# First FFN of a decoder layer: the second chunk's norm begun with the first, and weight and operand sums queued on POOL

## The chip, the cores and the metric

The kernel runs on one core of one Trainium2 chip. The metric is the time of one launch in device microseconds. Three runs of the kernel before took 2373.49, 2369.26 and 2369.44 us (median 2369.44). The profiled execution is a run of its own.

## What is computed

One inference step of a decoder layer in float32, for 1024 prompt tokens and 64 sample tokens together (1088 columns, model width 1024):

```python
def swiglu(x, w_gu, w_down):
    gate, up = jnp.split(x @ w_gu, 2, axis=-1)
    return (jax.nn.silu(gate) * up) @ w_down

def macaron_half(x, g_pre, w_gu, w_down, g_post):
    return x + 0.5 * rmsnorm(swiglu(rmsnorm(x, g_pre), w_gu, w_down), g_post)
...
hp = macaron_half(hp, ffn1...)        # first FFN, width 2752
...                                   # projections, two kinds of attention, w_out
hp = macaron_half(hp, ffn2...)        # second FFN
```

The change lies at the start of the first `macaron_half`: its RMS norm over the 1024 rows of a column, and the products with `w_gu` that follow it.

## The kernel before

Activations lie transposed: 8 row blocks of 128 partitions, tokens along the free axis. The 1088 columns are cut in four chunks, `CH` = 256, 256, 256 and 320 columns. The first two are one half (512 columns, tiles `y0` and, normed and split, `ua`), the last two the other (576 columns, `y1` and `ub`). The first FFN runs over the first half (`f1a` in the code) and then over the second (`f1b`).

Each float32 operand of a product is split in two parts, high (`wh`, `uh`, `hh`; a cast on ACT) and low (`wl`, `ul`, `hl`; a subtraction on DVE; in the norm every second row block's on POOL), and a product is three matmuls: high by high, high by low, low by high. The split of weights is `split`, lines 195 and 196. Weights are loaded into two raw buffers (`wr`, line 118) and split into three pairs of buffers, which come free when TensorE has used them. `Feed.pump` loads and splits ahead.

A half begins with `job_first`. For each of its two chunks it makes three products (`gemm`, line 272, 72 matmuls of 256 columns): the tail block of gate and up together, one gate block, one up block. For the first chunk this needs `norm0`, for the second the second chunk's norm. Then come four `down` products (line 530, 40 matmuls of 512 columns in the first half), which need `wt`, a small rearranged piece of the down weights (lines 678 and 679). Their results are copied over `y0` (line 542).

The next blocks are made in `sevens` by a scheme of seven smaller products in place of eight (`seven`, line 591). It needs two kinds of sums. Weight sums are made in `Sums.load` on POOL: three at line 89 and a fourth at line 94 for each block. Operand sums are made in the generator `sevens`, eight for each half at line 666, in place in the normed `y`, each followed by a split into free room: on DVE for the first half, on POOL for the second half (`f.early`), and on DVE for the second FFN's second half (`f3`). They must be through before the `down` results are copied over `y0`.

The norm of a chunk: `rms_quick` squares the eight blocks on ACT and DVE together, adds them to three partial sums, and TensorE adds these over partitions into `ncol` (line 323). The usual way is `square` (lines 282, 286 and 288) and line 301. `rms_col` makes the mean on DVE (line 331) and the power on POOL (line 332); `rms_diag` (343) and `rms_rows` (350) spread the result over partitions; then each block is scaled (412), cast (414) and its low part taken (415). Only the first chunk goes by `rms_quick`; the second is loaded whole in `first1` and its squares are begun after the first chunk's scaling was written.

The order of work on an engine is that in which a scheduler of the compiler issues what is written, moved by its own model of times; each engine then runs its queue strictly in order. `issue_after(x)` holds back instructions behind instruction x if they are on x's engine, and has no effect on other engines. Side work (`beside`) is written between matmuls at set distances.

Of the kernel before, what the change touches and what calls it, by code (L numbers as in the profile page):

```python
# [51 lines left out]
def run(g):  # L52
    for _ in g:
        pass
# [13 lines left out]
class Sums:  # L68
# [8 lines left out]
    def load(self, s):  # L77
        if self.first is self:
# [8 lines left out]
            for out, a, b, op in ((y[:, lo], a21, z[:, hi], ALU.add), (x[:, hi], y[:, lo], x[:, lo], ALU.subtract),  # L87
                                  (y[:, hi], x[:, lo], a21, ALU.subtract)):
                nc.gpsimd.tensor_tensor(out=out, in0=a, in1=b, op=op)  # L89
            self.tiles = [(x, 2 * h), (y, 2 * h), (z, 2 * h), (s4, h)]  # L90
# [7 lines left out]
class Feed:  # L98
# [8 lines left out]
    def _raw(self):  # L107
# [8 lines left out]
        for p in pieces:  # L116
            n = p.shape[-1]
            nc.sync.dma_start(t[:, o:o + n], p)
            o += n
        self.raws.append((t, o))  # L120

    def _split(self):
# [44 lines left out]
class Step:  # L167
# [136 lines left out]
    def rms_quick(self, y, n, pool):  # L304

        nc = self.nc
        wn = windows(n)
        col = self.ptile("col2")[:, :8]
        sq = []
        for k in range(KB):  # L310
# [7 lines left out]
            for a, b in ((0, 2), (1, 3), (4, 5), (6, 7), (6, 4)):  # L318
                if k == max(a, b, 7 * (a == 6)):
                    (nc.vector if a else nc.gpsimd).tensor_tensor(out=sq[a], in0=sq[a], in1=sq[b], op=ALU.add)  # L320
        for i in (0, 1, 6):
            for j, o in enumerate(wn):
                nc.tensor.matmul(col[:, 2 * j:2 * j + 2], sq[i][:, o:o + P], self.ones[:, :2], start=(i == 0 and j == 0), stop=(i == 6 and j == len(wn) - 1))
        return self.rms_col(col, len(wn), pool)

    def rms_col(self, col, m, pool):

        nc = self.nc
        v = pool.tile([P, 4], F32, name=self.uid("nv"), tag="nv", bufs=6)
        vs = v[:, :m]  # L330
        nc.vector.tensor_scalar(vs, col.rearrange("p (j c) -> p j c", c=2)[:, :m, 0], 1.0 / D, EPS, op0=ALU.mult, op1=ALU.add)
        nc.gpsimd.tensor_tensor(out=vs, in0=vs, in1=self.mhalf[:, :m], op=ALU.pow)
        return vs
# [24 lines left out]
    def norm(self, y, y0, c0, n, pool, post=None, pre=None, v=None, key=None):  # L358
# [49 lines left out]
        for k in range(KB):  # L408
# [5 lines left out]
            nc.scalar.copy(uh, yk)  # L414
            (nc.gpsimd if k % 2 else nc.vector).tensor_tensor(out=ul, in0=yk, in1=uh.bitcast(F32), op=ALU.subtract)
        self.ready.add((key, c0))
# [21 lines left out]
    def ffn(self, w_gu, w_dn, f):  # L438
# [216 lines left out]
        def sevens():  # L655
# [7 lines left out]
            for nm, out, p, q in (("t1", b11, b12, b11), ("t3", b12, b22, b12), ("t2", b22, b22, b11), ("t4", b21, b21, b22)):  # L663
                for h in (slice(0, 2), slice(2, 4)):
                    with self.tc.issue_after(self.mark):
                        (nc.gpsimd if f.early else nc.vector).tensor_tensor(out=out[:, h], in0=p[:, h], in1=q[:, h], op=ALU.subtract)
                    yield 1.0
# [519 lines left out]
class StepB(StepA):  # L1187
# [428 lines left out]
    def whole(self):  # L1616
# [21 lines left out]
        for k, m in ((0, 2), (2, 2), (4, 4)):  # L1638
            nc.sync.dma_start(y0[:, k:k + m, :CH[0][1]], A["xT"][:, k:k + m, :CH[0][1]])
        nc.sync.dma_start(self.gain, A["gains"])  # L1640
        for i in (1, 5):
            nc.vector.tensor_scalar(self.gain[:, i, :], self.gain[:, i, :], 0.5, None, op0=ALU.mult)
# [19 lines left out]
        def first1(i):  # L1662
            if i == 0:
                c0, n = CH[1]
                nc.sync.dma_start(y0[:, :, c0:c0 + n], A["xT"][:, :, c0:c0 + n])
                self.load_a()
                run(norm0)
            self.need(("f1", CH[i][0]))
            if i == 0:
                self.beside(self.norm(y0, 0, *CH[1], F, pre=0, key="f1"))  # L1670

# [120 lines left out]
        def after2(c0, n, v):  # L1792
# [14 lines left out]
                  after=lambda c0, n, v: self.norm(p4.y, HALF, c0, n, p4.R, (5, self.h2, O["yT"]), None, v))  # L1807

        sums(f3, flata, lambda: p3.y, lambda: self.need(("o", CH[1][0])))
        f3.first = lambda i: self.need(("f2", CH[2 + i][0]))  # L1810

        def start5():
# [3 lines left out]
            self.px, _ = self.pool("px", keep=True, space=PSUM)  # L1816
        norm0 = self.norm(y0, 0, *CH[0], F, pre=0, key="f1", v=[self.rms_quick(y0, CH[0][1], F)])
        next(norm0)
# [99 lines left out]
```

## Time and profile before

| | before |
|---|---|
| runs, median of 3 (lowest to highest) | 2369.44 us (2369.26 to 2373.49) |
| profiled execution, time | 2357.24 us |
| its span | 2355.5 us |
| TensorE (PE) busy | 2260.2 us, 96% |
| DVE busy | 1558.4 us, 66% |
| ACT busy | 1035.5 us, 44% |
| POOL busy | 710.1 us, 30% |

The profiled execution takes 1.7 us more than its span, and it is 12.2 us shorter than the median of the runs. Busy times of engines overlap. Time without work on TensorE lies mostly at the span's start, at the changes from one part to the next, and at the end.

### The profile page before, as it was taken

How to read it: one execution, taken by the hardware profiler on the slowest of the kernel's cores; microseconds unless marked ns; L12 is line 12 of the kernel's file. 1: busy time of each engine (PE TensorE's matmuls, PEld its weight loads, DVE VectorE, ACT ScalarE, POOL GpSimd, SP SyncE). 2: the span in 40 equal slices, each digit the busy share in tenths (PEclk: the TensorE clock that was granted, in tenths of full speed). 3: DMA queues.
4: the chain of work that ended last, by engine and by line, in shares of the span. 5: the costliest groups of instructions: out<-in, count | busy, mean ns of one | idle time of the engine just before them, and what ended most of it. 6: DMA issues, size and time to landing. Idle time of an engine off the chain costs nothing.

```text
span 2355.5 us, 41285 instructions
## 1 busy us (share of the span) xinstructions
PE 2260.2 (96%) x15512; PEld 2006.8 (85%) x15512; DVE 1558.4 (66%) x2723; ACT 1035.5 (44%) x1786; POOL 710.1 (30%) x658
## 2 busy tenths in 40 slices
PE   6999999999999989999999999999999998999997
PEld 5999988999999869999997666667777988999997
DVE  7888867877777774566465332339675689778765
ACT  5444434533344555755454222226556555334332
POOL 3444415433323221011124444631010135333402
PEclk8999999999999999999999999999999999999998
DMA  4332333322234556664357998865555544433212
GB/s 148 103 97 94 98 122 115 100 89 90 90 105 143 167 191 207 187 199 138 106 184 247 331 316 295 278 190 154 145 156 149 188 157 157 148 95 99 81 59 85
DMA packets 203337, 359.40 MB, mean 153 GB/s; under 512 B 27969, under 2 KB 105858, under 8 KB 202882
## 3 DMA queue, kind: packets, MB, share of 16 engines
q1 hardware_dynamic: 191474, 318.48, 43.4%
q0 software_dynamic: 11664, 38.28, 4.7%
q8 instruction: 123, 2.02, 0.4%
q14 instruction: 76, 0.62, 0.1%
HBM read 311.02 MB, written 45.65 MB: 151 GB/s over the span
## 4 chain that ended last, share of the span: by engine, by line
PE 65%; DVE 16%; issue 6%; ACT 5%; DMA 5%; POOL 3%; SPq 1%; DVEq 0%; POOLq 0%; ACTq 0%
PE mm L272 21%; PE mm L530 17%; PE mm L591 16%; DVE wl L196 6%; ACT wh L195 2%; DMA wr<-in_wout 2%; PE po L1084 2%; PE po L1294 1%; PE sp L1046 1%; PE tp L1278 1%; PE pa L1427 1%; DVE y L606 1%; PE mx L591 1%; DMA y<-in_xT 1%; DMA wr<-in_wgu 1%
## 5 line engine op out<-in xcount | busy, mean ns | idle before, releaser
L272 PE MATMUL mm<-ua,wh 128*128 128x512 f32 (+2 forms) x1712 | 461.1, 358 | 9.0 <-ACT wh L195 6.0
L196 DVE TENSOR_TENSOR wl<-wr,wh 128x1024 fp32r<-128x1024 f32 (+1 forms) x257 | 298.3, 1161 | 169.1 <-ACT wh L195 166.7
L195 ACT CAST wh<-wr 128x1024 fp32r<-128x1024 f32 (+1 forms) x257 | 250.1, 974 | 298.8 <-PE mm L272 101.7
L272 PEld LDWEIGHTS mm<-ua,wh 128*128 128x128 f32 (+1 forms) x1712 | 293.0, 193 | 66.8 <-issue 25.0
L530 PE MATMUL mm<-hh,wh 128*128 128x320 f32 (+2 forms) x974 | 326.9, 339 | 13.7 <-DVE y L544 6.0
L530 PE MATMUL mm<-hl,wh 128*128 128x256 f32 (+2 forms) x1022 | 336.8, 331 | 0.3 <-DVE hl L196 0.2
L272 PE MATMUL mm<-ub,wh 128*128 128x320 f32 (+2 forms) x1600 | 334.9, 304 | 2.0 <-DVE y L544 2.0
L530 PE MATMUL mm<-hh,wl 128*128 128x320 f32 (+2 forms) x974 | 320.4, 330 | 0.9 <-DVE wl L196 0.9
L272 PE MATMUL mm<-ua,wl 128*128 128x512 f32 (+1 forms) x848 | 294.5, 348 | 1.1 <-DVE wl L196 1.1
L591 PE MATMUL mm<-ub,wh 128*128 128x288 f32 (+1 forms) x1392 | 269.9, 290 | 0.9 <-DVE sg L606 0.9
L272 PEld LDWEIGHTS mm<-ub,wh 128*128 128x128 f32 (+1 forms) x1600 | 256.4, 189 | 9.4 <-issue 7.9
L272 PE MATMUL mm<-ub,wl 128*128 128x320 f32 (+1 forms) x784 | 233.0, 297 | 0.7 <-DVE wl L196 0.7
L544 DVE TENSOR_TENSOR y<-y,mm 128x320 f32<-128x320 f32 (+2 forms) x291 | 143.1, 519 | 128.6 <-PE mm L530 128.2
L591 PEld LDWEIGHTS mm<-ub,wh 128*128 128x128 f32 x1392 | 220.8, 189 | 1.1 <-issue 1.1
L530 PEld LDWEIGHTS mm<-hh,wh 128*128 128x128 f32 x974 | 185.1, 191 | 40.0 <-DVE y L544 9.1
L591 PE MATMUL mm<-ua,wh 128*128 128x288 f32 (+1 forms) x1104 | 215.0, 290 | 3.2 <-DVE up L606 2.4
L530 PEld LDWEIGHTS mm<-hl,wh 128*128 128x128 f32 x1022 | 195.5, 191 | 15.0 <-issue 1.3
L591 PE MATMUL mm<-ub,wl 128*128 128x288 f32 (+1 forms) x696 | 201.8, 290 | 0.0
L530 PEld LDWEIGHTS mm<-hh,wl 128*128 128x128 f32 x974 | 185.5, 191 | 16.8 <-DVE wl L196 2.6
L89 POOL TENSOR_TENSOR y<-y,wz 128x512 f32<-128x512 f32 x52 | 68.6, 1319 | 427.9 <-DVE wl L196 422.2
L272 PEld LDWEIGHTS mm<-ua,wl 128*128 128x128 f32 x848 | 163.3, 193 | 22.0 <-DVE wl L196 2.0
L591 PEld LDWEIGHTS mm<-ua,wh 128*128 128x128 f32 x1104 | 175.4, 189 | 4.1 <-DVE up L606 2.6
(299 smaller groups left out, 4331.3 us busy)
## 6 DMA issues: line engine op xcount, KB each, us to landing
wr<-in_wgu SPq DMA_DIRECT2D x68, 512.0 KB
wr<-in_wd SPq DMA_DIRECT2D x64, 512.0 KB
pr<-in_ck SPq DMA_DIRECT2D x112, 256.0 KB
wz<-in_wgu SPq DMA_DIRECT2D x104, 256.0 KB
wr<-in_win SPq DMA_DIRECT2D x50, 512.0 KB
wr<-in_wout SPq DMA_DIRECT2D x32, 512.0 KB
y<-in_wgu SPq DMA_DIRECT2D x52, 256.0 KB
wx<-in_wgu SPq DMA_DIRECT2D x52, 256.0 KB
```

The costliest lines, as they stand in the source:

```text
L89: nc.gpsimd.tensor_tensor(out=out, in0=a, in1=b, op=op)
L195: self.keep(self.nc.scalar.copy(hi, src))
L196: self.keep(self.nc.vector.tensor_tensor(out=lo, in0=src, in1=hi.bitcast(F32), op=ALU.subtract))
L272: nc.tensor.matmul(out, a, x[:, k, o:o + n], start=(k == 0 and j == 0), stop=(k == KB - 1 and j == len(ops) - 1))
L530: nc.tensor.matmul(pds[key], a, x, start=(i == 0 and j == 0), stop=(i == len(g) - 1 and j == len(ops) - 1))
L544: nc.vector.tensor_tensor(out=yk, in0=yk, in1=pds[d2, c0, e], op=ALU.add)
L591: nc.tensor.matmul(ps, a, x, start=(k == 0 and j == 0), stop=(k == KB // 2 - 1 and j == len(ops) - 1))
L606: add = lambda out, x, y: self.keep(nc.vector.tensor_tensor(out=out, in0=x, in1=y, op=ALU.add))
L1046: nc.tensor.matmul(sp[32 * a:32 * a + 32, 256 * hf:256 * hf + 256], qz[p % 2][:, a, s, :], raw[:, :, a * P:(a + 1) * P], start=False, stop ...
L1084: nc.tensor.matmul(po[r], pT[:, t, r], raw[:, :, a * P:(a + 1) * P], start=(t == 0), stop=False)
L1278: nc.tensor.transpose(tp[:, k * P:(k + 1) * P], p[:, (k0 + k) * P:(k0 + k + 1) * P], self.ident)
L1294: nc.tensor.matmul(out, v[:, k, r], pT[:, k, s], start=(k == 0 or (k == 1 and not one)), stop=(k == last or (k == last - 1 and not one)))
```

## The change

The second chunk's columns are loaded right behind the first weight block, in two transfers of four row blocks. `rms_quick` is cut in two: squares and partial sums are written at once, and the rest (matmuls over partitions, mean, power) is a function `finish`, called after the first two blocks of the first chunk are scaled. DVE's part of the second chunk's squares is held behind the first chunk's mean. The weight sums on POOL are held behind `low`, the last low part of the newest norm, which is a POOL instruction. The operand sums of both halves of the first FFN go to POOL behind the same instruction; those of `f3` stay on DVE, where `low` holds nothing.

```diff
 # Sums.load, Feed._raw
+                with s.tc.issue_after(s.low):
+                    nc.gpsimd.tensor_tensor(out=out, in0=a, in1=b, op=op)
...
+        s.behind_raw.pop(len(self.raws), lambda: None)()
...
 # rms_quick
-        for i in (0, 1, 6):
-            for j, o in enumerate(wn):
-                nc.tensor.matmul(col[...], sq[i][:, o:o + P], self.ones[:, :2], ...)
-        return self.rms_col(col, len(wn), pool)
+        def finish():
+            col = self.ptile("col2")[:, :8]
+            ...                                   # the same matmuls
+            return self.rms_col(col, len(wn), pool)
+        return finish
...
 # rms_col, norm
+        self.mean = nc.vector.tensor_scalar(vs, ...).ins
...
+            low = (nc.gpsimd if k % 2 else nc.vector).tensor_tensor(out=ul, ...)
+        self.low = low.ins
...
 # sevens
-                    with self.tc.issue_after(self.mark):
-                        (nc.gpsimd if f.early else nc.vector).tensor_tensor(out=out[:, h], ...)
+                    with self.tc.issue_after(self.mark), self.tc.issue_after(self.low):
+                        (nc.vector if f is self.third else nc.gpsimd).tensor_tensor(out=out[:, h], ...)
...
 # whole
+        def fetch1():
+            c0, n = CH[1]
+            for k in (0, 4):
+                nc.sync.dma_start(y0[:, k:k + 4, c0:c0 + n], A["xT"][:, k:k + 4, c0:c0 + n])
+        self.behind_raw = {1: fetch1}
...
         def first1(i):
             if i == 0:
+                self.load_a()
                 c0, n = CH[1]
-                nc.sync.dma_start(y0[:, :, c0:c0 + n], A["xT"][:, :, c0:c0 + n])
-                self.load_a()
+                with tc.issue_after(self.mean):
+                    finish = self.rms_quick(y0[:, :, c0:c0 + n], n, F)
+                next(norm0)
+                next(norm0)
+                norm1 = self.norm(y0, 0, *CH[1], F, pre=0, key="f1", v=[finish()])
+                next(norm1)
                 run(norm0)
+                self.beside(norm1)
             self.need(("f1", CH[i][0]))
-            if i == 0:
-                self.beside(self.norm(y0, 0, *CH[1], F, pre=0, key="f1"))
```

## Rows read from the trace of the kernel before

**Rows 1.** The page's busy line: busy us, share of the span, instructions.
```profile
PE 2260.2 (96%) x15512; PEld 2006.8 (85%) x15512; DVE 1558.4 (66%) x2723; ACT 1035.5 (44%) x1786; POOL 710.1 (30%) x658
```

**Rows 2.** TensorE by stretch: us, length, busy (matmuls), granted clock, DMA share, GB/s.
```profile
14.50:23.50 9.00, 8.83 (x57) 1.00 0.79 242
...
54.80:61.20 6.40, 6.31 (x21) 0.73 0.07 26
```

**Rows 3.** TensorE's timeline: start, busy us, instruction, count, idle before and releaser.
```profile
22.92 0.40 PE L272 MATMUL mm<-ua,wh 128*128 128x256 f32 x2
23.16 0.28 PE L272 MATMUL mm<-ua,wl 128*128 128x256 f32 x1
26.20 0.58 PE L301 MATMUL ncol<-ones,ss 128*128 128x2 f32 x4 [2.76 <-DVE ss L286]
...
29.79 1.22 PE L350 MATMUL nrows<-dg,ones 128*128 128x128 f32 x4 [1.60 <-DVE dg L343]
...
44.68 0.47 PE L530 MATMUL mm<-hh,wt 128*128 128x512 f32 x1 [2.36 <-DVE wt L679]
...
54.89 0.47 PE L530 MATMUL mm<-hh,wt 128*128 128x512 f32 x1 [3.78 <-DVE wt L679]
...
60.95 0.39 PE L530 MATMUL mm<-hh,wl 128*128 128x512 f32 x1
61.19 0.39 PE L591 MATMUL mm<-ua,wh 128*128 128x256 f32 x2
```

**Rows 4.** POOL's timeline, 22 to 37 us.
```profile
22.91 1.46 POOL L89 TENSOR_TENSOR y<-y,wz 128x512 f32<-128x512 f32 x1
...
28.57 0.71 POOL L332 TENSOR_TENSOR nv<-nv,mhalf 128x2 f32<-128x2 f32 x1
...
35.94 0.74 POOL L415 TENSOR_TENSOR ua<-y,ua 128x256 fp32r<-128x256 f32 x1 [0.31 <-ACT ua L414]
```

**Rows 5.** DVE's timeline, 18 to 65 us.
```profile
18.89 1.83 DVE L415 TENSOR_TENSOR ua<-y,ua 128x256 fp32r<-128x256 f32 x2
...
31.05 1.26 DVE L412 SCALAR_TENSOR_TENSOR y<-y,gain,nrows 128x256 f32<-128x256 f32 x3 [1.32 <-PE nrows L350]
...
54.45 0.49 DVE L679 CAST wt<-wl 64x256 fp32r<-64x256 f32 x2
...
62.28 2.17 DVE L196 TENSOR_TENSOR wl<-wz,wh 128x1024 fp32r<-128x1024 f32 x1 [1.55 <-ACT wh L195]
```

**Rows 6.** Groups by line and shape, DVE's L666 from 20 to 62 us, the others whole.
```profile
L666 DVE TENSOR_TENSOR y<-y 128x512 f32<-128x512 f32 x8 | 5.8, 731 | 0.0
...
L196 DVE TENSOR_TENSOR wl<-wx,wh 128x1024 fp32r<-128x1024 f32 x52 | 63.4, 1218 | 8.6 <-ACT wh L195 8.6
...
L89 POOL TENSOR_TENSOR y<-wx,y 128x512 f32<-128x512 f32 x52 | 102.5, 1971 | 0.6 <-DMA wx<-in_wgu 0.6
L89 POOL TENSOR_TENSOR wx<-y,wx 128x512 f32<-128x512 f32 x52 | 89.1, 1713 | 0.1
L89 POOL TENSOR_TENSOR y<-y,wz 128x512 f32<-128x512 f32 x52 | 68.6, 1319 | 427.9 <-DVE wl L196 422.2 <-issue 4.8 <-DMA y<-in_wgu 0.9
L94 POOL TENSOR_TENSOR y<-wz,wx 128x512 f32<-128x512 f32 x52 | 68.4, 1316 | 74.2 <-issue 40.0 <-POOL wx L89 25.2 <-DMA wz<-in_wgu 4.9
L666 POOL TENSOR_TENSOR y<-y 128x576 f32<-128x576 f32 x8 | 13.2, 1666 | 0.5
```

**Rows 7.** The second half's start, from the timelines of TensorE, POOL and ACT.
```profile
383.21 1.97 PE L530 MATMUL mm<-hh,wh 128*128 128x512 f32 x4 [2.01 <-ACT hh L195]
...
395.83 1.54 POOL L415 TENSOR_TENSOR ub<-y,ub 128x320 fp32r<-128x320 f32 x1 [1.06 <-ACT ub L414]
397.45 3.81 POOL L666 TENSOR_TENSOR y<-y 128x576 f32<-128x576 f32 x2
...
420.74 1.05 ACT L195 CAST wh<-wx 128x1024 fp32r<-128x1024 f32 x1
```

**Rows 8.** A later stretch: us, length, busy of PE, PEld, DVE, ACT, POOL; clock, DMA.
```profile
1300.00:1350.00 50.00, 49.74 (x327) 32.21 (x325) 16.06 (x24) 14.21 (x19) 24.48 (x24) 1.00 0.93 323
```

More of the change, by code (lines that the diff above doesn't have):

```diff
@@ L88, in load @@
                                   (y[:, hi], x[:, lo], a21, ALU.subtract)):
-                nc.gpsimd.tensor_tensor(out=out, in0=a, in1=b, op=op)
+                with s.tc.issue_after(s.low):
+                    nc.gpsimd.tensor_tensor(out=out, in0=a, in1=b, op=op)
             self.tiles = [(x, 2 * h), (y, 2 * h), (z, 2 * h), (s4, h)]
@@ L307, in rms_quick @@
         wn = windows(n)
-        col = self.ptile("col2")[:, :8]
         sq = []
@@ L320, in rms_quick @@
                     (nc.vector if a else nc.gpsimd).tensor_tensor(out=sq[a], in0=sq[a], in1=sq[b], op=ALU.add)
-        for i in (0, 1, 6):
-            for j, o in enumerate(wn):
-                nc.tensor.matmul(col[:, 2 * j:2 * j + 2], sq[i][:, o:o + P], self.ones[:, :2], start=(i == 0 and j == 0), stop=(i == 6 and j == len(wn) - 1))
-        return self.rms_col(col, len(wn), pool)
+        def finish():
+            col = self.ptile("col2")[:, :8]
+            for i in (0, 1, 6):
+                for j, o in enumerate(wn):
+                    nc.tensor.matmul(col[:, 2 * j:2 * j + 2], sq[i][:, o:o + P], self.ones[:, :2], start=(i == 0 and j == 0), stop=(i == 6 and j == len(wn) - 1))
+            return self.rms_col(col, len(wn), pool)
+        return finish
     def rms_col(self, col, m, pool):
@@ L330, in rms_col @@
         vs = v[:, :m]
-        nc.vector.tensor_scalar(vs, col.rearrange("p (j c) -> p j c", c=2)[:, :m, 0], 1.0 / D, EPS, op0=ALU.mult, op1=ALU.add)
+        self.mean = nc.vector.tensor_scalar(vs, col.rearrange("p (j c) -> p j c", c=2)[:, :m, 0], 1.0 / D, EPS, op0=ALU.mult, op1=ALU.add).ins
         nc.gpsimd.tensor_tensor(out=vs, in0=vs, in1=self.mhalf[:, :m], op=ALU.pow)
@@ L414, in norm @@
             nc.scalar.copy(uh, yk)
-            (nc.gpsimd if k % 2 else nc.vector).tensor_tensor(out=ul, in0=yk, in1=uh.bitcast(F32), op=ALU.subtract)
+            low = (nc.gpsimd if k % 2 else nc.vector).tensor_tensor(out=ul, in0=yk, in1=uh.bitcast(F32), op=ALU.subtract)
+        self.low = low.ins
         self.ready.add((key, c0))
@@ L664, in sevens @@
                 for h in (slice(0, 2), slice(2, 4)):
-                    with self.tc.issue_after(self.mark):
-                        (nc.gpsimd if f.early else nc.vector).tensor_tensor(out=out[:, h], in0=p[:, h], in1=q[:, h], op=ALU.subtract)
+                    with self.tc.issue_after(self.mark), self.tc.issue_after(self.low):
+                        (nc.vector if f is self.third else nc.gpsimd).tensor_tensor(out=out[:, h], in0=p[:, h], in1=q[:, h], op=ALU.subtract)
                     yield 1.0
@@ L1807, in whole @@
                   after=lambda c0, n, v: self.norm(p4.y, HALF, c0, n, p4.R, (5, self.h2, O["yT"]), None, v))
+        self.third = f3
         sums(f3, flata, lambda: p3.y, lambda: self.need(("o", CH[1][0])))
@@ L1816, in start5 @@
             self.px, _ = self.pool("px", keep=True, space=PSUM)
-        norm0 = self.norm(y0, 0, *CH[0], F, pre=0, key="f1", v=[self.rms_quick(y0, CH[0][1], F)])
+        norm0 = self.norm(y0, 0, *CH[0], F, pre=0, key="f1", v=[self.rms_quick(y0, CH[0][1], F)()])
         next(norm0)
```

## The prediction

> **What bounds the kernel now.** I read the page first. TensorE is busy for 96% of the span and no other engine for more than 66% [rows 1], so what a change is worth is the time in which TensorE stands still, or runs at its lower clock, and no longer does. I then read TensorE's timeline, wait by wait, at the two places that the diff touches.
>
> At the start of the first half its matmuls begin to flow at about 14.5 us, run without a gap to 23.44 us, and then stop four times [rows 2, 3]: 2.76 us for the second chunk's sums of squares, 1.60 us for the diagonal of its root, and 2.36 and 3.78 us for `wt`, DVE's cast of a piece of the down weights. Each stop also costs clock: in the 6.4 us behind the last one the granted clock is 0.73 [rows 2], a mixture of 1.2 and 2.4 GHz, with TensorE idle before it. The first of the seven products starts at 61.19 us [rows 3]. That start is my yardstick: whatever it moves is the gain of this stage.
>
> POOL's timeline shows why the second chunk is late. Four weight sums are queued from 22.91 us on, and the power of that chunk's mean starts only behind them, at 28.57 us; the last POOL split of the chunk ends at 36.68 us [rows 4]. DVE's timeline has the scaling of that chunk beginning at 31.05 us, though the first chunk's last split on DVE ended at 20.72 us [rows 5]. So some ten microseconds lie between the two chunks.
>
> **The change part by part.** *The second chunk's norm.* Its squares take no new work: five on ACT, three on DVE and four sums, in place of a chain of eight squares and seven sums. What the trace can't show is when they fit. The first chunk's DVE queue has its last split ending at 20.72 us; I add one split of a weight block, 1.22 us [rows 6], because the first weight load to come behind the new transfers lands later and its split then falls among the scaling. Lower bound of this cost nothing, upper bound that split. The second chunk's scaling then starts near 21.9 us. From the start of its scaling to its last POOL split it took 36.68 - 31.05 = 5.63 us [rows 4, 5], so `low` ends at about 27.6 us, 9.1 us sooner than before.
>
> *TensorE's bound.* It had done 57 of the first chunk's matmuls at 23.44 us [rows 2, 3]. With no wait, 15 more and the second chunk's 72 follow at 0.12 us (two in 0.24 us, 22.92 to 23.16) [rows 3]: 10.4 us. The new sum over partitions has 12 matmuls, at 0.58 / 4 us each 1.7 us; spreading the root takes 1.2 us [rows 3]. That puts the end of the six products at 36.8 us. The 40 down matmuls at 0.24 us (60.95 to 61.19) [rows 3] take 9.6 us: 46.4 us.
>
> *Weight and operand sums on POOL.* The eight operand sums were 5.8 us of DVE [rows 6]. POOL takes 1.666 us for 576 columns, so I estimate 1.48 us for 512, 11.9 us for eight. The four weight sums have means of 1.32, 1.71, 1.97 and 1.32 us, together 6.3 us [rows 6]. All twelve stand behind `low`: 27.6 + 18.2 = 45.8 us. If the operand sums go first, the first seven-product still needs the weights cast and split, 1.05 us on ACT [rows 7] and 1.22 us on DVE [rows 6]: 48.1 us. If the weight sums go first, the operands come last; what then waits is the copy of the down products over `y0`, with TensorE's banks behind it, to about the same time. POOL's bound is later than TensorE's by 1.7 us, so I take it: 48.1 us in place of 61.19 us, a gain of 13.1 us. At the uncontended 1.32 us for all twelve POOL would end at 43.4 us, and TensorE's 46.4 us would count: 14.8 us.
>
> *`wt`.* Where two casts stood behind other DVE work until 54.45 us [rows 5], DVE now has 5.8 us less to do. I cost this wait at nothing; the cover is that DVE room, and the price if it is gone is rival A.
>
> *The second half.* Its operand sums were on POOL already, mixed with the chunk's low parts; the last two ended at 401.26 us. Now all eight stand behind the last low part, which ended at 397.37 us [rows 7]: 8 x 1.67 = 13.3 us, to 410.7 us, and the weight sums 6.3 us more, to 417.0 us. The cast of these weights stood at 420.74 us [rows 7], so there are 3.7 us of room. On the other side, TensorE waited 2.01 us at 383.21 us for ACT [rows 7], whose queue had an operand's cast that waited for POOL; that goes, if ACT no longer meets a late sum there. From a gain of 2.0 us to a loss of 9.4 us (410.7 - 401.3), I take nothing, by the room.
>
> *Transfers.* The second chunk's megabyte goes ahead of the second weight block. That block serves the second product, and the squares need the chunk; the 1.22 us above is what I charge. SP's later loads shift with it and are taken up by the wait behind `low`. The holds in the second FFN's second half cost nothing: its operand sums stay on DVE, and its weight sums already follow the norm.
>
> *Does the gain last?* Where DMA is busiest, at 0.93, TensorE still works 49.74 of 50 us [rows 8]: nothing there is tied to a fixed time, so an earlier start moves it all.
>
> **Sum.** 13.1 us from the profiled execution's 2357.24 us gives 2344.1 us. The runs lie 12.2 us above that execution; I subtract the same gain from their median, 2369.44 us: 2356.3 us.
>
> **Rivals.** *A: DVE gets no room, and the `wt` waits stay.* POOL's sums slow DVE's subtractions of two operands beside them: the split of `wz` at 62.28 us took 2.17 us where one beside an idle POOL takes 1.22 us [rows 5, 6]. Eight moved sums that each hold up one such split cost DVE 8 x 0.95 = 7.6 us for the 5.8 us saved. The stage from the last of the six products to the first seven-product then stays 61.19 - 42.32 = 18.9 us (42.32 is 44.68 less its wait) [rows 3], from 36.8 us on: 55.7 us, a gain of 5.5 us, 2363.9 us. Against it speaks the second half, where sums on POOL stand beside `wt` with no such gap. The Trainium skill, "SBUF — State Buffer", section "Who interferes with whom", says that a DVE instruction with two SBUF inputs contends with a GpSimd instruction that reads SBUF, since both need a read interface that is locked for a whole instruction; the 2.17 us row agrees, and by that rule A would be the likeliest case.
>
> *B: the change doesn't bring the second chunk forward.* If its partial sums stand behind the first chunk's scaling on DVE and the root comes as late as now, only the order on POOL changes: 36.68 + 18.2 + 2.3 = 57.2 us, a gain of 4.0 us, 2365.4 us. For it: DVE is full from 14 to 21 us. Against it: only about 3 us of DVE work is asked for, and the first chunk's root leaves a hole before its scaling.
>
> *C: slower. ACT and DVE, in order, stand behind POOL's sums.* In the second half they would meet sums 9.4 us later than now, or 15.7 us if the weight sums go first, with TensorE's results waiting in its banks for the same two engines. In the first half the down products would start only behind the sums, at 45.8 us, and end at 55.4 us, a gain of 5.8 us. The net is 3.6 to 9.9 us slower; at the middle 6.8 us, 2376.2 us. It decides when the second half's stop exceeds 10.5 us (5.8 and the 4.7 us that can be told). Against it: the order is made with the sums' times in view.
>
> **How the numbers follow.** Within 0.2%, 4.7 us, a measurement of this kernel can't tell a change. Forecast 0.58 (its own range 2352 to 2360 us), A 0.16, B 0.14, C 0.12. A lies less than a microsecond inside the bound for faster, so I count 0.10 of it as faster and 0.06 as same. Faster 0.68, same 0.20, slower 0.12. The range goes down to 2350 us (TensorE's bound, the 2.0 us of the second half and some 2 us more, for the rewarmed clock there) and up to 2370 us, no change at all; C lies above it.
>
> **What would show it.** Right: `ncol` of the second chunk by line 323 with a wait under 1 us, its scaling from about 22 us, line 666 on POOL after 27 us, the `wt` waits gone, and line 591 starting at 46 to 50 us. A shows as waits for `wt` with DVE splits near 1 us longer; B as scaling after 28 us; C as ACT or DVE waiting on line 666 with TensorE waiting for them, above all from 397 to 425 us. The prediction is wrong if line 591 starts early but the span does not shrink with it.

## The result, and the profile after

The changed kernel is slower. Its median is 2380.81 us (2372.05 to 2385.72, 20 runs) against 2373.88 us (2367.47 to 2378.19, 20 runs) for the kernel before on the same chip: a ratio of 1.0031 [1.0023, 1.0039], that is 7.4 us more [5.5, 9.3] (the medians stand 6.9 us apart), where 13.1 us less were forecast.

The two profiled executions stand 27.5 us apart (2384.71 and 2357.24 us), and that distance is not the effect. A second profiled execution of the kernel before, below, took 2369.97 us: 12.7 us more than its first, with the same program. From 460 us on, every engine has its instructions in the same order before and after. So I read the two places that the change touches, each by its own length.

The yardstick of the prediction, the first of the seven products (line 591 before, 596 after), starts at 62.64 us in place of 61.19 us [rows 3]. TensorE's timeline of the kernel after, with idle time and releaser in brackets:

```profile
12.80 1.01 PE L326 MATMUL ncol<-ones,sq 128*128 128x2 f32 x4 [2.67 <-POOL sq L321]
15.78 1.02 PE L326 MATMUL ncol<-ones,sq 128*128 128x2 f32 x4 [0.26 <-DVE sq L321]
16.66 2.10 PE L274 MATMUL mm<-ua,wh 128*128 128x256 f32 x4
24.55 0.60 PE L354 MATMUL nrows<-dg,ones 128*128 128x128 f32 x4
43.39 0.76 PE L535 MATMUL mm<-hh,wt 128*128 128x512 f32 x1 [3.76 <-DVE wt L684]
46.35 0.76 PE L535 MATMUL mm<-hh,wt 128*128 128x512 f32 x1 [0.92 <-DVE wt L684]
52.21 1.22 PE L535 MATMUL mm<-hh,wh 128*128 128x512 f32 x2 [4.24 <-ACT hh L197]
62.64 0.40 PE L596 MATMUL mm<-ua,wh 128*128 128x256 f32 x2
...
416.18 0.55 PE L535 MATMUL mm<-hh,wt 128*128 128x256 f32 x1 [3.02 <-DVE wt L684]
...
429.97 0.42 PE L596 MATMUL mm<-ub,wh 128*128 128x288 f32 x2
```

The two stops for the second chunk's norm (2.76 and 1.60 us [rows 3]) are gone, as meant. The six products end at 43.39 - 3.76 = 39.63 us in place of 42.32. All of that, and more, is given back at the down matmuls: three stops of 8.92 us, where two of 6.14 us were, and some 1.4 us more in the matmuls between and behind the stops. The last of the three names a new releaser, ACT's cast `hh`. POOL's timeline shows what moved in beside these matmuls:

```profile
32.59 0.74 POOL L419 TENSOR_TENSOR ua<-y,ua 128x256 fp32r<-128x256 f32 x1 [0.31 <-ACT ua L418]
33.29 4.43 POOL L671 TENSOR_TENSOR y<-y 128x512 f32<-128x512 f32 x3
37.68 1.74 POOL L90 TENSOR_TENSOR y<-y,wz 128x512 f32<-128x512 f32 x1
...
46.02 5.89 POOL L671 TENSOR_TENSOR y<-y 128x512 f32<-128x512 f32 x4
...
392.62 12.92 POOL L671 TENSOR_TENSOR y<-y 128x576 f32<-128x576 f32 x8
```

The twelve sums stand as one block behind `low`, from 33.29 to 51.91 us. ACT's timeline shows who stands behind them: of the eight casts of these operands six wait for their sums, and `hh`, which needs no sum, comes only at 51.75 us, behind four that waited.

```profile
26.13 1.28 ACT L461 ACT_TABLE_LOAD   x1
...
44.42 0.62 ACT L197 CAST ub<-y 128x512 fp32r<-128x512 f32 x1 [3.61 <-POOL y L671]
47.37 0.62 ACT L197 CAST ub<-y 128x512 fp32r<-128x512 f32 x1 [2.03 <-POOL y L671]
...
50.71 0.62 ACT L197 CAST ub<-y 128x512 fp32r<-128x512 f32 x1 [1.05 <-POOL y L671]
51.75 0.40 ACT L197 CAST hh<-sg 128x256 fp32r<-128x256 f32 x1
...
402.78 0.67 ACT L197 CAST ua<-y 128x576 fp32r<-128x576 f32 x1 [0.72 <-POOL y L671]
403.48 0.38 ACT L461 ACTIVATE sg<-mm 64x256 f32<-64x256 f32 x1
```

ACT's list of waits from 30 to 60 us (total, times, longest) sums them up:

```profile
ACT ub L197 <- POOL y L671: 10.0, 6, 3.6
```

DVE's timeline has the third effect. Its subtractions of two operands that both lie in SBUF take about twice their time beside most of POOL's sums: 1.77 us at 36.49 us, where 0.69 us is usual (one, at 41.30 us, took 0.68 us there too). Even the small cast `wt` takes 1.26 us. `sg`, with one operand from TensorE (`mm`), keeps its 0.42 us. The cast in the profile before:

```profile
44.24 0.29 DVE L679 CAST wt<-wl 64x256 fp32r<-64x256 f32 x1
```

DVE in the profile after:

```profile
22.75 0.41 DVE L419 TENSOR_TENSOR ua<-y,ua 128x256 fp32r<-128x256 f32 x1
25.19 1.26 DVE L416 SCALAR_TENSOR_TENSOR y<-y,gain,nrows 128x256 f32<-128x256 f32 x3 [2.03 <-PE nrows L354]
...
36.49 1.77 DVE L198 TENSOR_TENSOR wl<-wr,wh 128x512 fp32r<-128x512 f32 x1
...
41.98 1.26 DVE L684 CAST wt<-wl 64x256 fp32r<-64x256 f32 x1
...
46.24 0.42 DVE L466 TENSOR_TENSOR sg<-mm,sg 128x256 f32<-128x256 f32 x1
...
403.89 0.43 DVE L466 TENSOR_TENSOR sg<-mm,sg 64x256 f32<-64x256 f32 x1 [6.62 <-ACT sg L461]
...
415.75 0.29 DVE L684 CAST wt<-wl 64x256 fp32r<-64x256 f32 x1
```

The same rows show `sg`, the operand of `hh`, done at 46.66 us: ACT's cast of it stood 5.1 us in its queue.

The second half has one block too, eight sums from 392.62 to 405.54 us, with the activation `sg` behind casts that wait for them, DVE idle for 6.62 us until that `sg`, and a new stop of TensorE, 3.02 us, at 416.18 us. The length from the last matmul that spreads the second half's root (line 350 before, 376.71 us; 378.37 us after) to that half's first seven-product was 49.53 us; it is 51.60 us now. The same places in the profile before, of ACT, DVE and TensorE:

```profile
401.99 0.38 ACT L456 ACTIVATE sg<-mm 64x256 f32<-64x256 f32 x1
```
```profile
412.55 0.76 DVE L679 CAST wt<-wl 64x256 fp32r<-64x256 f32 x1
```
```profile
413.77 0.28 PE L530 MATMUL mm<-hh,wt 128*128 128x256 f32 x1
```

Counted from the root, `sg` is not later: 25.3 us before, 25.1 us after. But `wt` ends at 36.6 us before and 37.7 us after, because the same thirteen DVE instructions from `sg` to `wt` take 12.2 us in place of 10.9 us: more of them run beside POOL's sums. TensorE, on its side, reaches these matmuls sooner, at 34.8 us in place of 37.1 us, as the stop of 2.01 us for `hh` [rows 7] is gone. So it stops for `wt`, and from that stop to the seven-product it takes 13.8 us, where it took 12.5 us, at a granted clock of 0.78 in place of 1.00.

So the profile of after shows 1.45 us lost in the first half's opening and 2.07 us in the second's.

### The profile page after: what moved, and what is told of

It reads as the page before. It is cut to its first block, busy times and chain, and to the rows that moved or that the text cites. A ratio compares the mean times of both kernels' runs of the same rounds, so it can differ in the third digit from the quotient of the medians.

```text
span 2382.9 us, 41300 instructions
## 1 busy us (share of the span) xinstructions
PE 2272.4 (95%) x15520; PEld 2011.9 (84%) x15520; DVE 1558.5 (65%) x2717; ACT 1035.0 (43%) x1783; POOL 726.2 (30%) x665
## 3 DMA queue, kind: packets, MB, share of 16 engines
q1 hardware_dynamic: 191490, 318.48, 42.6%
q8 instruction: 123, 2.02, 0.4%
## 4 chain that ended last, share of the span: by engine, by line
PE 63%; DVE 15%; issue 7%; DMA 5%; ACT 5%; POOL 3%; SPq 1%; another core or an unknown queue 1%; DVEq 0%; POOLq 0%; ACTq 0%
PE mm L274 19%; PE mm L535 17%; PE mm L596 15%; DVE wl L198 5%; ACT wh L197 2%; PE po L1089 2%; DMA wr<-in_wout 1%; PE po L1299 1%; PE sp L1051 1%; PE tp L1283 1%; PE pa L1432 1%; DVE y L611 1%; PE mx L596 1%; POOL y L671 1%; DMA y<-in_xT 1%
```

## The experiments

Each kernel ran beside the kernel before on the same chip; the ratios are to that. Times in the table are of each kernel's one profiled execution, in us: *first* is the start of the first seven-product, *second* the length just defined, and *load* the distance from the issue of the second half's columns to the third weight cast on ACT behind it, which enters late in the series.

| kernel | first | second | load | ratio [95%] |
|---|---|---|---|---|
| before | 61.19 | 49.53 | 11.56 | |
| before, again | 61.00 | 49.53 | 10.48 | one run |
| after | 62.64 | 51.60 | 11.71 | 1.0031 [1.0023, 1.0039] |
| after, again | 63.12 | 52.83 | 12.48 | 1.0041 [1.0027, 1.0056] |
| 1 operand sums back | 61.42 | 49.56 | 12.55 | 1.0017 [1.0003, 1.0031] |
| 2 norm alone | 58.02 | 49.59 | 13.1 | 0.9999 [0.9988, 1.0011] |
| 3 sums and hold alone | 62.35 | 51.37 | 10.51 | 1.0020 [1.0008, 1.0033] |
| 4 hold alone | 65.23 | 49.53 | 11.06 | 1.0007 [0.9995, 1.0020] |
| 5 after without the hold | 58.33 | 51.02 | 12.92 | 1.0016 [1.0005, 1.0026] |
| 6 norm, `wt` on POOL | 54.69 | 49.56 | 12.63 | 0.9981 [0.9971, 0.9991] |
| 7 hold, sums as fills | 59.74 | 49.54 | 11.93 | one run |
| 8 second half's sums back | 61.61 | 49.54 | 12.68 | one run |
| 10 as 6, one transfer | 53.24 | 49.54 | 12.53 | 0.9980 [0.9966, 0.9994] |
| 11 as 6, mean late | 56.05 | 49.51 | 12.5 | 0.9986 [0.9976, 0.9995] |
| 12 early transfer alone | 59.87 | 49.53 | 12.01 | 1.0004 [0.9989, 1.0019] |
| 13 norm, old transfer | 56.91 | 49.53 | 10.69 | 0.9985 [0.9971, 0.9999] |
| 14 `wt` on POOL alone | 55.74 | 49.57 | 12.13 | 0.9986 [0.9975, 0.9998] |
| 15 13 and 14 | 54.54 | 49.54 | 10.65 | 0.9977 [0.9962, 0.9993] |

*First* varies by 0.2 to 0.5 us between two executions of one kernel, *second* by nothing before and by 1.2 us after.

**1: the operand sums as before; norm and weight hold stay.**

```diff
-with self.tc.issue_after(self.mark), self.tc.issue_after(self.low):
-    (nc.vector if f is self.third else nc.gpsimd).tensor_tensor(...)
+with self.tc.issue_after(self.mark):
+    (nc.gpsimd if f.early else nc.vector).tensor_tensor(...)
```

> The changed kernel with the operand sums placed as before the change (first half on DVE, second half on POOL, neither held behind the norm); the early norm and the held weight sums stay. Theory T (the loss comes from ACT's and DVE's queues, which run in order and stand behind operand sums that POOL makes late): the 4.2 us stop of TensorE for a cast of the last hidden block goes, the second half is no longer 2.3 us later, the first seven-product starts at 52 to 57 us, and the time falls below before by 4 to 9 us. Rival R (the early norm itself costs: its sums over partitions stand in front of the first products, and its squares push back the first chunk's scaling): the first seven-product starts at 60 us or later and the time is within 2 us of before or above it.

The second half came back whole (49.56 us), so its loss is the operand sums'. The first half did not: 61.42 us, where 52 to 57 had been expected. The operand sums alone were not what kept the early norm from paying.

**2: the norm alone (1, and the weight sums not held).**

```diff
-                with s.tc.issue_after(s.low):
-                    nc.gpsimd.tensor_tensor(out=out, in0=a, in1=b, op=op)
+                nc.gpsimd.tensor_tensor(out=out, in0=a, in1=b, op=op)
```

> Only the early norm and the early load of the second chunk, on the kernel before; no sum on POOL is moved or held. T: the second chunk is scaled earlier, but the weight sums may stand in front of its power on POOL, 5.7 us at most; first seven-product at 52 to 60 us, 2 to 9 us faster than before, and not faster than with the weight sums held. R: no gain, first seven-product at 60 us or later.

58.02 us: 3.2 us sooner than before, and 3.4 us sooner than 1, where no gain over 1 was expected. The hold is what 1 lost: 1 has a stop of 3.36 us for `wt` at 42.27 us, behind four DVE instructions that are each some 1.1 us longer, and 2 has none there. A stop for `wt` of 4.96 us stays in both:

```profile
51.32 0.77 PE L534 MATMUL mm<-hh,wt 128*128 128x512 f32 x1 [4.96 <-DVE wt L683]
58.02 0.39 PE L595 MATMUL mm<-ua,wh 128*128 128x256 f32 x2
```

The runs don't show the 3.2 us: 0.9999.

**3: operand sums and hold, with the norm as before.** On the kernel before:

```diff
 # Sums.load, Feed._raw, norm: as 4, below
 ...
 # sevens
-with self.tc.issue_after(self.mark):
-    (nc.gpsimd if f.early else nc.vector).tensor_tensor(...)
+with self.tc.issue_after(self.mark), self.tc.issue_after(self.low):
+    (nc.vector if f is self.third else nc.gpsimd).tensor_tensor(...)
```

> Only the sums: the operand sums of both halves on POOL behind the last low part, the weight sums held there too, with the norm as before the change. T: slower than before by 3 to 9 us, the second half 2 us later than before by itself, and in the first half ACT waiting for line 666 on POOL with TensorE waiting for ACT. R: no more than 1 us of difference from before in either half, since the cost would lie in the early norm.

Slower without any early norm: 62.35 and 51.37 us, 1.0020. ACT waits 7.7 us for POOL's sums, as expected, but TensorE does not stop for ACT there: it waits 6.10 us for `wt` and 2.65 us for `hl`, both DVE's.

**4: the weight hold alone.** On the kernel before. The order on DVE and ACT stays that of the kernel before, and on TensorE only the matmuls that spread the second chunk's root change their place among the products.

```diff
 # Sums.load, Feed._raw
-                nc.gpsimd.tensor_tensor(out=out, in0=a, in1=b, op=op)
+                with s.tc.issue_after(s.low):
+                    nc.gpsimd.tensor_tensor(out=out, in0=a, in1=b, op=op)
...
 # norm
+            low = (nc.gpsimd if k % 2 else nc.vector).tensor_tensor(out=ul, ...)
+        self.low = low.ins
```

> Only the weight sums held behind the last low part of the norm, nothing else. The power of the second chunk's mean no longer stands behind four weight sums. T: it comes up to 5 us sooner, the 1.6 us stop for the diagonal shrinks, and the first seven-product starts 1 to 5 us sooner. R (POOL's order does not matter there, since the second chunk's sums of squares set the time): less than 1 us.

A gain of 1 to 5 us was expected, and the stage lost 4.0 us: 65.23 us. There was little to gain: in the profile before, DVE's mean of the second chunk (the line below) ended only at 27.66 us, and the power ran at 28.57 us [rows 4], so the weight sums held it up by 0.9 us and no more. It runs at 27.67 us here.

```profile
27.50 0.16 DVE L331 TENSOR_SCALAR nv<-ncol 128x2 f32<-128x2 f32 x1
```

Four sums that moved from 23 to 28.6 us to 36.0 to 42.6 us did that alone. TensorE, POOL and DVE of this kernel:

```profile
47.50 0.76 PE L532 MATMUL mm<-hh,wt 128*128 128x512 f32 x1 [6.45 <-DVE wt L681]
...
65.23 0.39 PE L593 MATMUL mm<-ua,wh 128*128 128x256 f32 x2
```
```profile
36.01 1.74 POOL L90 TENSOR_TENSOR y<-y,wz 128x512 f32<-128x512 f32 x1
...
40.98 1.59 POOL L95 TENSOR_TENSOR y<-wz,wx 128x512 f32<-128x512 f32 x1
```
```profile
36.52 1.51 DVE L197 TENSOR_TENSOR hl<-sg,hh 128x256 fp32r<-128x256 f32 x1
37.96 1.78 DVE L668 TENSOR_TENSOR y<-y 128x512 f32<-128x512 f32 x1
39.66 1.79 DVE L197 TENSOR_TENSOR wl<-wr,wh 128x512 fp32r<-128x512 f32 x1
41.37 1.75 DVE L197 TENSOR_TENSOR ub<-y,ub 128x512 fp32r<-128x512 f32 x1
...
43.60 0.69 DVE L197 TENSOR_TENSOR ub<-y,ub 128x512 fp32r<-128x512 f32 x1
```

As long as POOL sums here, each DVE subtraction of 512 columns takes 1.75 to 1.79 us, about as long as a POOL sum; when POOL is done, 0.69 us again. With the 1.51 us of `hl` (0.41 before) these are four delays of some 1.1 us, and the stop for `wt` grew by 4.09 us (2.36 to 6.45). Two readings were left: the engines take turns, or the late weight sums hold up a tile that DVE needs.

**5: the change without the hold** (the edit of 2 alone, on the kernel after).

> The changed kernel without the hold on the weight sums; the operand sums stay on POOL behind the last low part. Theory P (POOL's sums slow DVE's subtractions of two SBUF operands beside them, one for one): with the four weight sums out of the 33 to 52 us stretch, DVE's subtractions there have a mean nearer to 0.7 us by four collisions of 1 us, and the first seven-product starts 3 to 5 us sooner than in the changed kernel, at 57.5 to 60 us. Theory T (ACT and DVE in order behind late operand sums): the operand sums come 7 us sooner and the 4.2 us stop goes; about the same start, but with DVE's durations unchanged. Rival R (neither matters): 62 us or later.

58.33 us: the hold costs 4.3 us here too. Theories P and T both expected such a start, and the durations tell them apart. Lines of POOL, ACT and DVE:

```profile
33.67 12.78 POOL L670 TENSOR_TENSOR y<-y 128x512 f32<-128x512 f32 x8
```
```profile
47.09 0.41 ACT L196 CAST hh<-sg 128x256 fp32r<-128x256 f32 x1 [1.14 <-DVE sg L465]
```
```profile
36.87 1.79 DVE L197 TENSOR_TENSOR wl<-wr,wh 128x512 fp32r<-128x512 f32 x1
```

DVE's instructions up to 46.6 us are as long as in the kernel after, since the operand sums stand beside them now; only two splits behind that are shorter, 1.28 us in place of 2.98 us. What goes is the stop of 4.24 us: POOL's block ends at 46.45 us in place of 51.91 us, and ACT's cast `hh` follows `sg` at once. So with the operand sums on POOL the hold costs mostly by POOL's and ACT's queues, as T had it. Beside 2, the run shows what moving the operand sums is worth in the first half: 58.33 against 58.02, nothing, for 5.8 us less on DVE. ACT's waits for POOL's sums are 3.9 us here, none in 2, and the stops for `wt` are 5.99 us, 4.96 us in 2. The ratio, 1.0016, is still a loss, with 1.5 us of it in the second half.

**7: turns or late tiles.** As 4, with each of the first block's four weight sums replaced by three fills of its output, which only write; these four sums are left out.

```diff
 # Sums.load, on 4; s.blocks counts the blocks begun
-                    nc.gpsimd.tensor_tensor(out=out, in0=a, in1=b, op=op)
+                    if s.blocks:
+                        nc.gpsimd.tensor_tensor(out=out, in0=a, in1=b, op=op)
+                    for _ in range(0 if s.blocks else 3):
+                        nc.gpsimd.memset(out, 0.0)
...
 # the fourth sum in the same way
```

> The kernel with nothing but the weight sums held, and the first block's four weight sums left out: in place of each, three fills of the same tile on POOL, behind the same instruction, which write and read nothing. The orders of DVE, ACT and TensorE are the same as with the sums. Theory P (a POOL sum that reads two operands takes turns with DVE's subtractions of two operands): DVE's subtractions of 512 columns between 36 and 43 us take 0.7 us again in place of 1.75 us, the wait for wt falls from 6.5 us to 2.4 us or less, and the first seven-product starts at 60 to 61.5 us in place of 65.2 us. Theory H (any work of POOL at that time slows DVE, or the held tiles themselves come too late): 64 us or later.

POOL, DVE and TensorE of this kernel: nine of the fills keep POOL busy for 4.5 us of the same stretch, behind the same hold, and DVE does not notice.

```profile
35.71 0.53 POOL L93 MEMSET y<- 128x512 f32 x1
...
38.51 1.70 POOL L93 MEMSET y<- 128x512 f32 x3
```
```profile
36.58 0.68 DVE L676 TENSOR_TENSOR y<-y 128x512 f32<-128x512 f32 x1
37.18 0.68 DVE L205 TENSOR_TENSOR wl<-wr,wh 128x512 fp32r<-128x512 f32 x1
37.78 0.68 DVE L205 TENSOR_TENSOR ub<-y,ub 128x512 fp32r<-128x512 f32 x1
```
```profile
43.21 0.77 PE L540 MATMUL mm<-hh,wt 128*128 128x512 f32 x1 [2.37 <-DVE wt L689]
...
59.74 0.40 PE L601 MATMUL mm<-ua,wh 128*128 128x256 f32 x2
```

The stop for `wt` is 2.37 us, that of the kernel before, and the yardstick, 59.74 us, a little under the 60 to 61.5 us expected. So in 4 it is the sums' reading beside DVE's two operands that costs, and not POOL's being busy or the tiles' being late.

**8: the second half's operand sums not held** (on the kernel after).

```diff
-with self.tc.issue_after(self.mark), self.tc.issue_after(self.low):
+with self.tc.issue_after(self.mark), self.tc.issue_after(self.mark if f.early else self.low):
```

> The changed kernel with the second half's operand sums not held (still on POOL, as before the change); the first half as changed. T: from the last spreading of the second half's root to its first seven-product 49.5 to 49.8 us as in the kernel before, in place of 51.6 and 52.8 us; the first half stays at 62 to 63.5 us. Rival: 51 us or more, if the weight sums held there or the shifted loads are the cause.

49.54 us, with the old stop for `hh` back (2.02 us): the hold of eight sums alone is the second half's loss.

**6: the stop for `wt`.** Kernel 2, with the lower half of `wt` cast on POOL in the first half, where POOL has nothing else then.

```diff
-nc.vector.tensor_copy(wt[64:, :], ...)
+(nc.gpsimd if f.raw else nc.vector).tensor_copy(wt[64:, :], ...)
```

> The early norm alone, and the low half of wt in the first half cast on POOL and not on DVE. In the early norm alone TensorE stops for 5.0 us at 46 us for that cast, which stands in DVE's queue behind a split that waits for TensorE. P and T alike: POOL is free there, the stop goes, the first seven-product starts at 53 to 55 us, 6 to 8 us sooner than before, and the time is 0.2 to 0.4% under before. R (the stop has another cause, such as the split of the weights themselves): 57 us or later.

54.69 us and 0.9981: faster than both kernels.

**The same kernels again.** Nothing is changed in these two; they show how far executions differ.

> The changed kernel once more, unaltered, with a profile of its own. Every stage on which the reading rests should come back: the first seven-product at 62 to 63.5 us, the second half's 1 to 3 us later than before by itself. If the later parts (600 to 1550 us, where the first profile lay 20 us behind with the same order of instructions) come back with other distances, these are the spread of executions and not the change.

> The kernel before once more, unaltered, with a profile of its own: the first seven-product at 61.2 us within 0.5 us, and from there to the second half's within 1.5 us of 365.0 us; what differs in the later parts is the spread of executions.

After repeats its result (1.0041), with the same three stops in the first half (3.76, 0.91 and 4.23 us). The stages of before repeat within 0.2 us, while its span is 12.7 us longer. The length between the two seven-products, expected within 1.5 us of 365.0 us, was 362.8 us: a miss.

**10 to 13: where the rest goes.** The runs of after lose 7.4 us, the two stages of its profile 3.5. These kernels looked for the rest in the early transfer and the early mean. 10 is 6 with one transfer in place of two:

```diff
-            for k in (0, 4):
-                nc.sync.dma_start(y0[:, k:k + 4, c0:c0 + n], A["xT"][:, k:k + 4, c0:c0 + n])
+            nc.sync.dma_start(y0[:, :, c0:c0 + n], A["xT"][:, :, c0:c0 + n])
```

> The early norm with wt's low half on POOL, and the second chunk loaded by one transfer and not two (as many transfers in all as in the kernel before). The stages that the early norm touches gain 6.4 us by their profile, and the runs showed 4.5 us. If the one transfer more shifts which queue each later transfer takes, and costs 2 to 4 us that way in the later parts, the time falls by that much, to 0.996 to 0.997 of before. If not, it stays at 0.998, and the difference is the spread of executions.

0.9980, no different from 6: it isn't the additional transfer. 11 is 6 with the second chunk's sums over partitions, mean and power written behind the first matmuls, since the twelve `ncol` matmuls stand ahead of the first product:

```diff
-                next(norm0)
-                next(norm0)
-                norm1 = self.norm(y0, 0, *CH[1], F, pre=0, key="f1", v=[finish()])
-                next(norm1)
                 run(norm0)
-                self.beside(norm1)
+                v = []
+                def late():
+                    yield 1.0
+                    v.append(finish())
+                self.beside(late(), True)
+                self.beside(self.norm(y0, 0, *CH[1], F, pre=0, key="f1", v=v))
```

> The early norm with wt's low half on POOL, and the second chunk's sum over partitions, mean and power written behind the first matmuls of the first product, no longer ahead of them. The early norm's first product starts at 16.7 us, 2 us later than before, since eight matmuls of the second chunk's sums stand ahead of it on TensorE. With them behind it starts at 14.6 to 15.2 us, and the first seven-product 0.5 to 2 us sooner than 54.7 us, if the second chunk is still scaled before TensorE asks for it; if its power then comes late, 54.7 us or later, with a wait for the diagonal. Time 0.996 to 0.998 of before.

A miss, and no test of its reading: on TensorE the second chunk's twelve `ncol` matmuls ran ahead of the first product all the same (13.13 to 16.99 us), so that product did not start sooner, and the yardstick was later, 56.05 us. 12 is the kernel before with the early transfer and nothing else; 13 is kernel 2 with the transfer where the kernel before has it.

```diff
 # 12, on before
+        self.behind_raw = {1: fetch1}
...
-                nc.sync.dma_start(y0[:, :, c0:c0 + n], A["xT"][:, :, c0:c0 + n])
```
```diff
 # 13, on 2
-        self.behind_raw = {1: fetch1}
+        self.behind_raw = {}
...
         def first1(i):
             if i == 0:
+                fetch1()
```

> The kernel before with nothing but the second chunk's load moved: behind the first weight block, in two transfers. The norm stays as before. Theory L (the place of this load costs by itself, since the second weight block lands later, and something in the later transfers is shifted): 2 to 4 us slower than before, and from the issue of the second half's columns at about 337 us to the cast of the next weights 12 us or more, in place of 10.5 to 11.9 us in the kernels with the norm as before. Theory S (that distance and the rest of the loss are the spread of executions): within 1 us of before by the ratio, the distance 10.5 to 12 us.

> The early norm alone, with the second chunk loaded where the kernel before loads it, by one transfer. L: the distance from the issue of the second half's columns to the next cast falls to 10.5 to 12 us, and the kernel is 2 to 4 us faster than the early norm with the early load, at 0.998 to 0.999 of before; the first seven-product at 57 to 60 us, since the chunk lands 1 to 2 us later. S, or the early norm itself being the cause: 12.5 us or more, ratio 0.9990 to 1.0010.

The early transfer alone makes no difference that the runs show (1.0004), though its yardstick is 1.3 us sooner. With the old place the norm brings the yardstick to 56.91 us and, at last, shows in the runs (0.9985), with a load distance of 10.69 us. But 14 has the old transfer and a distance of 12.13 us, and 12 the early one and 12.01 us: the distance does not go with the transfer's place, and the reading that it carries the missing time fell.

**14 and 15.** 14 is the kernel before with the `wt` edit of 6 alone, 15 is 13 with it.

> The kernel before with nothing but the low half of wt in the first half cast on POOL. The two stops of 2.4 and 3.8 us for it become shorter by 1 to 4 us each; the first seven-product starts at 55 to 58 us in place of 61.1 us; nothing else moves, so the time is 0.9975 to 0.9985 of before. If the early norm's cost in the later parts is real, this comes out faster than the early norm with the same cast (0.9981) for a smaller gain at the start.

> The two edits that gained, together: the early norm with the second chunk loaded where the kernel before loads it, and wt's low half in the first half cast on POOL. No sum is held or moved. If their gains at the start add (4.2 and 5.3 us, less the part of the wt stops that the early norm had already taken), the first seven-product starts at 52 to 54.5 us, 6.5 to 9 us sooner than before, and the time is 0.9965 to 0.998 of before. If the later parts give some of it back whatever is gained at the start, as the runs so far hint, 0.998 to 0.9985.

The small cast alone brings the yardstick to 55.74 us and the ratio to 0.9986. Kernel 15 has the best ratio of all, 0.9977, 5.4 us under the kernel before (its interval overlaps those of 6, 10, 13 and 14), with 2.67 us of stops left at the down matmuls:

```profile
45.88 0.47 PE L534 MATMUL mm<-hh,wt 128*128 128x512 f32 x1 [0.53 <-ACT y L546]
50.58 0.47 PE L534 MATMUL mm<-hh,wt 128*128 128x512 f32 x1 [2.14 <-ACT wt L682]
54.54 0.40 PE L595 MATMUL mm<-ua,wh 128*128 128x256 f32 x2
```

## Why the prediction was wrong

Three steps failed: the end of `low`, the second chunk's last split, forecast at 27.6 us; the choice of the later of TensorE's and POOL's bounds, as if the two ran apart; and the cover of the `wt` wait, costed at nothing. The first seven-product started 14.5 us later than forecast. Of that, 5.7 us are the end of `low`, at 33.3 us. 0.4 us are the length of the twelve sums; they ended at 51.91 us, not at 45.8 us. The other 8.4 us are the way from there to the seven-product, 10.7 us and not 2.3 us, since 33 of the 40 down matmuls still stood behind `hh`.

**The second chunk's norm: right in kind, less in size.** Forecast as 9.1 us for `low`, it was 3.35 us there (36.68 us before, 33.33 us after). Its squares were costed at one weight split; the first chunk's last split on DVE ended at 23.16 us, not 21.9 us. Its scaling then waited 2.03 us for the spread root, which TensorE makes in order behind matmuls of the first product, and that product began at 16.66 us (14.61 us before) behind the new chunk's `ncol` matmuls: 25.19 us. From there to the last POOL split it took 8.14 us, not 5.63 us. ACT's table load (1.28 us at 26.13 us) and the first product's activations, which came ahead of the second chunk's casts before, now stand among them. For the stage the norm was worth 3.2 us on its own (2) and 4.3 us with the old place of the transfer (13).

**POOL's queue: its length was right.** 18.2 us were estimated for the twelve sums; they took 18.6 us.

**`wt`: the cover was gone.** DVE was to have 5.8 us more room. It has eight sums less, but the held weight sums and the moved operand sums now stand beside its subtractions, and 4.7 us of stops for `wt` are left. The hold, which I costed only as POOL time, is the largest loss of the change: 4.0 us alone (4), 3.4 us on the norm (1 against 2), 4.3 us on norm and operand sums (after against 5). In the first two that is rival A's mechanism: 7 shows it for 4, and 1 has the same long subtractions and the stop behind them. In the third it is mostly the mechanism of the next paragraph. A's price, still a gain of 5.5 us, was too low a cost: it counted the operand sums only, and left the four weight sums out. The rule named there, the Trainium skill, "SBUF — State Buffer", section "Who interferes with whom", has such a DVE instruction contend with a GpSimd instruction that reads SBUF, and not with one that only writes it. It fits on both sides: 1.75 us beside a sum that reads, 0.68 us beside a fill that only writes.

**ACT in order behind POOL: missed where it was a cost.** The forecast let the down matmuls follow the six products at 36.8 us, with POOL still summing until 45.8 us. They need `hh`, and `hh` stands on ACT behind casts that wait for POOL: 10.0 us of waits (3.9 without the hold, in 5), and TensorE's 4.24 us stop. In the kernel after this decides the first half: the `wt` stops ahead of it end before `hh` is there. That is rival C, which held the first half to a gain of 5.8 us by the same picture. The 5.8 us saved on DVE are given back too: even without the hold, moving the operand sums changes the first half by 0.3 us (5 against 2), within what one kernel's executions differ.

**The second half: nothing was forecast, 2.07 us were lost** (3.3 us in the second profile of after), inside the bounds of -2.0 and +9.4 us. The 2.0 us of the gaining side did come, and more than that was lost behind it. The 3.7 us of room were read at a weight cast at 420.74 us [rows 7]; what went late was nearer, `wt`, 1.1 us later from the root, by DVE's instructions beside the sums. ACT did stand behind POOL, as C says, but `sg` came no later than before, so that wait cost nothing by itself. The larger part of the loss, 1.3 us, lies in the matmuls behind the stop, at the lower granted clock.

**"The gain lasts", and what stays open.** In the two profiles of after the stages lose 3.5 and 5.2 us; the runs lose 7.4 us [5.5, 9.3] and 9.7 us [6.4, 13.3]. Kernels 1, 2 and 5 fall short in the same way, by 3 to 5 us: 2 gains 3.2 us in its stage and nothing in the runs, so there the prediction's last sentence, an early seven-product without a shorter span, came true. The kernels that keep the early transfer fall short by 2 to 5 us, those without it by -2.4 to 2.1 us, which points at the transfer; but 12, which has it alone, is 1.0004 with an interval of 0.0015, 3.6 us, to either side, too wide to tell, and neither its number of transfers (10) nor the load distance (13, 14) carries it. Nor is it, in 2, a lower clock: its runs have a mean granted clock of 0.987, those of the kernel before beside them 0.985. Single profiles can't tell: the length between the two places differs by 2.2 us in the two executions of before, and the spans by 12.7. The cause of these 2 to 5 us is not settled.

Of the rivals' chances, C's 0.12 held the sign; the time lies outside the range, on its side. That its 3.6 to 9.9 us cover the measured 7.4 us is luck: it added a first half 5.8 us ahead and a second half at least 9.4 us behind, and the halves lost 1.45 and 2.07 us. B did not happen: the scaling did come forward, from 31.05 to 25.19 us.

## What to carry to other kernels

A sum on an idle POOL isn't free when it reads SBUF beside DVE's two-operand work: four sums moved by 13 us into a dense stretch cost their stage 4 us, and a 64-row cast taken from DVE there gained 5 us. Before a sum moves to a slower engine, list what stands behind its reader on each in-order engine, since the cast that waits for it also delays the next activation, which needs no sum. Two bounds whose chains share such an engine don't combine by the later of the two.

## What the hardware showed that was not expected

- Beside POOL's sums, a DVE subtraction of 128x512 can take as long as the POOL instruction: 1.75 to 1.79 us for 0.69 in kernel 4, from 0.68 to 1.77 us in the kernel after. ACT's casts of 128x512 show no such growth (0.62 us beside POOL's sums at 44.42 and 47.37 us).
- A fill of 128x512 on POOL takes 0.53 us and costs DVE nothing (0.68 us beside it).
- DVE's cast of 64x256 takes 1.26 us beside POOL's sums for 0.29 us without (line 679 before, at 44.24 us), though it has one operand.
- Behind the last stop TensorE's granted clock was lower than before, 0.62 in the 6.4 us from 52.20 us against 0.73 [rows 2], a mixture of 1.2 and 2.4 GHz, after three stops in place of two. In the second half it was 0.78 for the 13.8 us behind the new stop of 3.02 us, and 1.00 in the same stretch before, without a stop.
- Two executions of the same program can differ by 12.7 us in 2,360, with both touched stages equal to 0.2 us. The longer one reached the second half's seven-product 2.4 us sooner, so 15.1 us lie behind it. Over the 29 runs of the kernel before that stood beside 12 to 14, the longer ones tended to have the lower mean granted clock (the shortest, 2364.04 us, 0.987; the longest, 2377.62 us, 0.984).
